# A fused trunk block: the output projection's rows split in place in a two-slot ring, the values of two head pairs copied together

## The chip, the cores and the metric

The kernel runs on one core of a Trainium2 chip. The metric is the device time of one execution in microseconds (us). Five engines work side by side, each through its own instructions in the order in which they stand in the program: TensorE (PE; its weight loads are listed apart as PEld), VectorE (DVE), ScalarE (ACT), GpSimd (POOL) and SyncE (SP), which in this kernel issues nearly all transfers. An instruction that waits holds up everything behind it on its engine.

## The reference

One layer over 1024 tokens of width 1024, all in float32. A normed input is projected, three mixers work on parts of the result, their outputs are joined and projected again, and a gated feed-forward part follows:

```python
h = rmsnorm(x, ln1[l]); z = h @ w_in[l]
y_pool, y_gla, y_fox = pool_mixer(...), gla_mixer(...), fox_mixer(...)
x = x + concat([y_pool, y_gla, y_fox]) @ w_o[l]
gate, up = split(rmsnorm(x, ln2[l]) @ w_gu[l])
x = x + (silu(gate) * up) @ w_down[l];  return rmsnorm(x, ln_f)
```

`fox_mixer` is a causal softmax attention with 8 heads of 64 columns. To each score a bias F_t - F_s is added, where F is a running sum of forget gates along the tokens; each head has its own row F.

## The kernel before

Every product keeps float32 accuracy with three matmuls: each operand is split into a high part (an ACT copy that rounds to fp32r) and a low part (a DVE or POOL subtraction, raw minus high), and high x high, high x low and low x high are summed in PSUM. So each block of weights costs a load, a copy and a subtraction before PE can use it.

The stages in order: norm and transposition of x (`hT`), the gated linear attention and the pooling (`Gla`, `pool_tile`), the attention (`fox_...`), the output projection in two halves (`pxa`, `pxb`, by `out_proj`), the feed-forward part (tiles `m`, L775), its down projection (tiles `d`, L1031), the last norm.

**The attention** works on four pairs of heads, p = 0 to 3. `fox_values(q)` (L518) projects the values for two pairs at once: 8 token blocks, `psv`, each 24 matmuls into a bank of the ring "gm", which has two banks, and then copies. `fox_qk(p)` projects queries and keys of one pair (`zq`, `zk`: 48 matmuls each in two banks "gm"). `fox_attend(p)` (L628) loads the bias row of each of the two heads, broadcast over 128 partitions (`fb`, L632), and then takes 8 items, a head `a` with two query blocks `m`: scores `s` on PE (three banks), bias and minimum by one DVE operation (L581), exponential on ACT (L585), scaling by POOL and DVE (L591, L593), transposition on PE (`pt`, L602), split on ACT and DVE (`pp`, L604 and L605), product with the values on PE (`o`, L616), sum of the two halves (L619, L622).

**The output projection's weights** are split early: `keep_wo(k)` (L280) loads 128 rows of `w_o` (512 KB), splits them and stores both parts to DRAM (`wod`); `fetch_wo` reads them back much later, for `out_proj`. In the Python text the eight calls stand between `fox_values(0)` and `fox_qk(0)`.

**Memory.** SBUF is cut into slots of 128 x 1024 floats. 33 of them go round as a queue: `G(name)` takes the slot that was freed longest ago, `free` puts slots back. The others form rings, from which `R(name, tag)` takes the next slot by turns: "p" 6, "pp" 3, "fb" 2, "wr" 2 (raw weights), "w" 4 (split weights). A tile that gets a slot waits until all users of the tile before it there are done. The ring "fb" holds the biases, and before the attention the norm's scratch and the rounded mixer outputs `mh`. `keep_wo` takes three tiles by `G` per call (raw, high, low), so that several calls can be under way at once.

**What sets the order.** The Python text gives the data flow and a priority. A scheduler of the tile framework lays all instructions out in advance, engine by engine, with its own estimate of durations; on the chip each engine then follows that fixed list. So a step can stand in the list far from its place in the text, and a change in one place moves others.

Of the kernel before, what the change touches and what calls it, by code (L numbers as in the profile page):

```python
# [10 lines left out]
F32R = mybir.dt.float32r  # L11
I8 = mybir.dt.int8
AF = mybir.ActivationFunctionType
ALU = mybir.AluOpType
# [4 lines left out]
P = 128  # L19
# [12 lines left out]
def tile_hybrid_block(ctx: ExitStack, tc, x, w_fv, w_gv, w_zt, w_o, w_gu, w_down, ln, w_pool, w_a3, chans, b_f, consts, out):  # L32
    nc = tc.nc
    ACT, DVE, POOL, PE, SP = nc.scalar, nc.vector, nc.gpsimd, nc.tensor, nc.sync
# [15 lines left out]
    def G(name, dtype=F32):  # L50
        i = idle.pop(0)
        t_ = big.tile([P, 1024], dtype, tag=f"g{i}", name=name)
        where[name] = i
        return t_

    def free(*names):
        for n in names:
            idle.append(where.pop(n))

    def R(name, dtype=F32, tag="p"):  # L60

        i = rings[tag].pop(0)
        rings[tag].append(i)
        return big.tile([P, 1024], dtype, tag=f"g{i}", name=name)
# [4 lines left out]
    def f(ap):  # L69
        return ap.bitcast(F32)  # L70
# [41 lines left out]
    def PS(tag, name):  # L112
        return pst.tile([P, 512], F32, tag=tag, name=name, bufs=BANKS[tag])
# [12 lines left out]
    def load_g(src, name, n=1024, eng=None, tag="wr"):  # L126
        if tag in rings:
            raw, own = R(f"{name}r", tag=tag), False
        else:
            raw, own = G(f"{name}r"), True  # L130
        r = split_w(src, raw, G(f"{name}h", F32R), G(f"{name}l", F32R), n, eng or DVE)
        if own:
            free(f"{name}r")
        return r
# [82 lines left out]
    for tb in range(NT):  # L217
# [4 lines left out]
        ps = PS("gm", f"psg{tb}")  # L222
# [45 lines left out]
    wod = dpool.tile([8, P, 2, D], F32, name="wod")  # L268
# [10 lines left out]

    def keep_wo(k):  # L280

        hi, lo = load_g(w_o[k * P:(k + 1) * P, :], f"wos{k}", tag="G")
        SP.dma_start(wod[k, :, 0], f(hi))
        SP.dma_start(wod[k, :, 1], f(lo))
        free(f"wos{k}h", f"wos{k}l")

    def fetch_wo(k):
        hl = G(f"wo{k}h", F32R), G(f"wo{k}l", F32R)
# [228 lines left out]

    def fox_values(q, smalls=((),) * NT):  # L518

        V = [[G(f"v{2 * q + j}_{i}", F32R).rearrange("p (t h s e) -> p t h s e", t=4, h=2, s=2) for i in range(2)] for j in range(2)]  # L520
        ws = [load_w(w_fv[:, q, i * 1024:(i + 1) * 1024], f"wfv{q}_{i}", eng=POOL) for i in range(2)]
        for tb in range(NT):
            ps = PS("gm", f"psv{q}_{tb}")
            woven(ps[:, 0:256], [(tok(hT, k, tb), tuple(w_[:, (k % 4) * 256:(k % 4) * 256 + 256] for w_ in ws[k // 4]))
                                 for k in range(NK)], smalls[tb])
            for j in range(2):
                v_ = V[j][tb // 4][:, tb % 4]
                pv = ps[:, 128 * j:128 * j + 128].rearrange("p (h e) -> p h e", h=2)
                ACT.activation(v_[:, :, 0], pv, AF.Copy)
                DVE.tensor_tensor(out=v_[:, :, 1], in0=pv, in1=f(v_[:, :, 0]), op=ALU.subtract)  # L530
        return V

    def fox_qk(p):
# [15 lines left out]

    def fox_item(p, a, m, ops, fb, V, Y):  # L550

        Q, K, KL = (t_[a] for t_ in ops)
        nm = f"{p}_{a}_{m}"
        rows = slice(64 * a, 64 * a + 64)
        Pb, Ws = [], []
        l, rl = S(f"l{nm}", 2), S(f"rl{nm}", 2)
        for i in range(2):
            qb = 2 * m + i
            W = P * (qb + 1)
            nh = 1 if W <= 512 else 2  # L560
            w = W // nh
            qs = slice(qb * P, (qb + 1) * P)
            mn = S(f"mn{nm}_{i}")
            if m >= 2:
                pb = R(f"pb{nm}_{i}")
            elif i == 0:
                pb2 = R(f"pb{nm}")
                pb = pb2[:, 0:512]
            else:
                pb = pb2[:, 512:1024]  # L570
            top = 3.0e38
            for h in range(nh):
                s = PS("s", f"s{nm}_{i}_{h}")
                ks = slice(h * w, (h + 1) * w)
                last = h == nh - 1
                PE.matmul(s[:, 0:w], Q[:, qs], K[:, ks], start=True, stop=False)  # L576
                PE.matmul(s[:, 0:w], Q[:, qs], KL[:, ks], start=False, stop=not last)  # L577
                if last:
                    PE.matmul(s[:, w - P:w], identr, maskr, start=False, stop=True)
                t_ = mn if last else S(f"mw{nm}_{i}")  # L580
                DVE.tensor_tensor_reduce(out=pb[:, ks], in0=s[:, 0:w], in1=fb[:, ks], scale=1.0, scalar=top,  # L581
                                         op0=ALU.add, op1=ALU.min, accum_out=t_)
                top = t_[:, 0:1]

            ACT.activation(pb[:, 0:W], pb[:, 0:W], AF.Exp, bias=mn[:, 0:1], scale=-1.0, accum_out=l[:, i:i + 1])  # L585
            Pb.append(pb)
            Ws.append(W)
        DVE.reciprocal(rl, l)  # L588
        for i, (pb, W) in enumerate(zip(Pb, Ws)):
            if i == 0:  # L590
                POOL.tensor_tensor(out=pb[:, 0:W], in0=pb[:, 0:W], in1=rl[:, 0:1].broadcast_to([P, W]), op=ALU.mult)  # L591
            else:
                DVE.tensor_scalar(out=pb[:, 0:W], in0=pb[:, 0:W], scalar1=rl[:, 1:2], scalar2=None, op0=ALU.mult)  # L593
        o = PS("o", f"o{nm}")
        for n in range(m + 1):
            pt = PS("pt", f"pt{nm}_{n}")
            pp = R(f"pp{nm}_{n}", F32R, tag="pp")
            cut = P if n == m else 0
            for b in range(2):
                for i in range(b if cut else 0, 2):  # L600
                    o0 = 256 * b + P * i - cut * b
                    PE.transpose(pt[:, o0:o0 + P], Pb[i][:, (2 * n + b) * P:(2 * n + b + 1) * P], ident)  # L602
            w = 512 - cut
            ACT.activation(pp[:, 0:w], pt[:, 0:w], AF.Copy)  # L604
            DVE.tensor_tensor(out=pp[:, 512:512 + w], in0=pt[:, 0:w], in1=f(pp[:, 0:w]), op=ALU.subtract)  # L605
            for b in range(2):
                kb = 2 * n + b
                o0 = cut * b
                v_ = V[p % 2][kb // 4][:, kb % 4, a]
                ph = pp[:, 256 * b:512 - o0] if b else pp[:, 0:256]  # L610
                pl = pp[:, 768:1024 - o0] if b else pp[:, 512:768]
                both = (o[:, o0:256], v_.rearrange("p s e -> p (s e)"), ph)
                high = (o[0:64, o0:256], v_[:, 0], pl)
                last = kb == 2 * m + 1
                for n_, args in enumerate((high, both) if last else (both, high)):
                    PE.matmul(*args, start=(kb == 0 and n_ == 0), stop=(last and n_ == 1))  # L616
        tmp = half(f"ot{nm}")
        ot, oy = tmp[0:64, 0:256], tmp[:, 256:512]
        ACT.activation(ot, o[64:128, 0:256], AF.Copy)  # L619
        if p < 3:  # L620
            oy = Y[:, m * 256:(m + 1) * 256]
        DVE.tensor_tensor(out=oy[rows], in0=o[0:64, 0:256], in1=ot, op=ALU.add)  # L622
        if p == 3:
            hi, lo = (last_mix[m // 2][rows, h, (m % 2) * 256:(m % 2 + 1) * 256] for h in range(2))
            ACT.activation(hi, oy[rows], AF.Copy)
            POOL.tensor_tensor(out=lo, in0=oy[rows], in1=f(hi), op=ALU.subtract)

    def fox_attend(p, ops, V, Y):  # L628
        fbs = []
# [4 lines left out]
        for a, m in ([(a, m) for a in range(2) for m in range(4)] if p < 3 else [(a, m) for m in (1, 0, 3, 2) for a in range(2)]):  # L634
            fox_item(p, a, m, ops, fbs[a], V, Y)

# [38 lines left out]
    V = fox_values(0, (B.within(1), o_[0][:1], o_[0][1:], o_[1][:1], o_[1][1:] + B.turned(0), B.turned(1), (), ()))  # L675
# [4 lines left out]
    for p in range(4):  # L680
        if p == 3:
            last_mix += [G(f"mix7_{g}", F32R).rearrange("p (h t) -> p h t", h=2) for g in range(2)]
        Y = G(f"y{p}") if p < 3 else None
        fox_attend(p, ops, V, Y)
        done = [f"{n}{p}_{a}" for n in ("q", "k", "kl") for a in range(2)] + [f"v{p}_{i}" for i in range(2)]
        if p == 1:
            V = fox_values(1)
            free(*[done.pop() for _ in range(2)])
        if p < 3:
            ops = fox_qk(p + 1)  # L690
        if p == 2:
            free(*names_T("hT"))
        if p < 3:
            free(*done)
            keep_mix(4 + p, Y)
            free(f"y{p}")
# [19 lines left out]
    raw = [[G(f"hr{q}_{kp}").rearrange("p (k t) -> p k t", k=2) for kp in range(2)] for q in range(4)]  # L716
# [407 lines left out]
```

## Time and profile before

| | |
|---|---|
| median of 3 runs | 1177.61 us (1175.17 to 1178.79) |
| the profiled execution | 1177.97 us |
| its span, first to last instruction | 1176.0 us |
| PE busy | 1136.7 us, 97% |
| DVE, ACT, POOL busy | 823.9, 537.0, 339.7 us |
| mean granted clock of PE | 0.992 |

The profile is one execution. A row of the timeline gives start, duration, engine, source line, operation and, in brackets, how long the engine sat idle before it and what ended the wait. A row of the table by windows gives a stretch of time and the busy time of each engine in it with its number of instructions, then the granted clock of PE, the share of the DMA engines that was busy, and GB/s. A DMA row gives the size and the median time from issue to landing.

### The profile page before, as it was taken

To read this page: it belongs to the slowest core of one execution; us is meant where nothing else is said; L and a number is where in the kernel's file an instruction comes from. 1 tells how busy PE (TensorE), PEld (TensorE's weight loads), DVE (VectorE), ACT (ScalarE), POOL (GpSimd) and SP (SyncE) were. 2 spreads that over 40 slices of the span, in tenths; PEclk is the share of its full clock that TensorE was granted. 3 is DMA by queue.
4 is the path that set the end of the run, shared out by engine and by line. 5 is a ranking of instruction groups with operands and counts; after the bars stand their busy time and mean duration, and the time that the engine had idled before them with its cause. 6 is when DMAs were issued, how large, how long until landed. Compare 5 with 4: busy or idle time off the path is not lost.

```text
span 1176.0 us, 15954 instructions
## 1 busy us (share of the span) xinstructions
PE 1136.7 (97%) x5928; PEld 959.4 (82%) x5928; DVE 823.9 (70%) x1365; ACT 537.0 (46%) x972; POOL 339.7 (29%) x260
## 2 busy tenths in 40 slices
PE   6999998999999999998999999999999999999996
PEld 6877878889978888886888888888888888888885
DVE  7596364287746866579997768777776684976686
ACT  6453344366654644456453434443343344334344
POOL 2131122443322313110202221022202271660693
PEclk9999999999999999999999999999999999999999
DMA  7111179311203734431333232332324688333233
GB/s 250 36 37 37 37 264 351 102 37 37 91 18 122 308 127 158 163 127 37 107 100 134 88 128 69 119 121 95 109 80 152 215 323 291 107 96 105 80 118 143
DMA packets 57692, 150.45 MB, mean 128 GB/s; under 512 B 5080, under 2 KB 5512, under 8 KB 57616
## 3 DMA queue, kind: packets, MB, share of 16 engines
q1 hardware_dynamic: 57184, 147.87, 36.8%
q0 software_dynamic: 432, 1.57, 0.4%
q8 instruction: 46, 0.75, 0.3%
q14 instruction: 30, 0.25, 0.1%
HBM read 105.09 MB, written 44.34 MB: 127 GB/s over the span
## 4 chain that ended last, share of the span: by engine, by line
PE 81%; DVE 7%; DMA 5%; POOL 3%; issue 2%; ACT 1%; SPq 0%; POOLq 0%; ACTq 0%; DVEq 0%
PE m L775 35%; PE d L1031 13%; PE pxa L144 4%; PE pxb L144 3%; PE o L616 3%; PE psv L152 2%; PE pt L602 2%; POOL rw L873 2%; PE s L576 1%; PE s L577 1%; PE zq3p L152 1%; PE psg L144 1%; PE zgk1p L152 1%; PE zgg0p L152 1%; PE zq2p L152 1%
## 5 line engine op out<-in xcount | busy, mean ns | idle before, releaser
L775 PE MATMUL m<-hA_0h,wr 128*128 128x512 f32 x616 | 214.2, 391 | 0.9 <-ACT hr L730 0.9
L775 PE MATMUL m<-hA_1h,wr 128*128 128x512 f32 x616 | 214.6, 389 | 0.0
L775 PEld LDWEIGHTS m<-hA_0h,wr 128*128 128x128 f32 x616 | 116.0, 188 | 25.3 <-ACT hr L730 1.4
L775 PEld LDWEIGHTS m<-hA_1h,wr 128*128 128x128 f32 x616 | 115.7, 188 | 23.9
L757 ACT ACTIVATE wr<-ws 128x512 fp32r<-128x512 f32 x110 | 69.2, 631 | 120.6 <-DVE ws L756 61.9
L775 PE MATMUL m<-hA_0l,wr 128*128 128x512 f32 x308 | 120.2, 390 | 0.7 <-DVE hA_0l L905 0.7
L1031 PE MATMUL d<-lw,ha 128*128 128x512 f32 x308 | 119.8, 389 | 0.0
L775 PE MATMUL m<-hA_1l,wr 128*128 128x512 f32 x308 | 119.8, 389 | 0.0
L1031 PE MATMUL d<-hw,ha 128*128 128x512 f32 x308 | 119.3, 389 | 0.0
L1031 PE MATMUL d<-hw,la 128*128 128x512 f32 x308 | 118.4, 389 | 0.0
L827 POOL TENSOR_TENSOR cg<-cu,cu 128x512 f32<-128x512 f32 x11 | 19.7, 1793 | 304.9 <-DVE cu L804 268.6
L758 DVE TENSOR_TENSOR wr<-ws,wr 128x512 fp32r<-128x512 f32 x110 | 75.6, 694 | 26.9 <-ACT wr L757 26.8
L881 DVE TENSOR_TENSOR la<-ra,ha 128x1024 fp32r<-128x1024 f32 (+1 forms) x42 | 57.5, 1375 | 30.1 <-ACT ha L880 22.4
L873 POOL TENSOR_TENSOR rw<-wd,wd 128x512 f32<-128x512 f32 x33 | 59.6, 1833 | 48.0 <-PE d L1031 47.9
L591 POOL TENSOR_TENSOR pb<-pb,rl 128x128 f32<-128x128 f32 (+3 forms) x32 | 39.3, 1232 | 115.2 <-DVE rl L588 105.1
L880 ACT ACTIVATE ha<-ra 128x1024 fp32r<-128x1024 f32 (+1 forms) x42 | 41.2, 987 | 65.6 <-DMA ra<-cd 60.6
L775 PEld LDWEIGHTS m<-hA_0l,wr 128*128 128x128 f32 x308 | 58.0, 188 | 13.2 <-DVE hA_0l L905 1.1
L585 ACT ACTIVATE pb<-pb,mn 128x128 f32<-128x128 f32 (+3 forms) x64 | 49.5, 774 | 41.1 <-DVE mn L581 39.8
L605 DVE TENSOR_TENSOR pp<-pt,pp 128x512 fp32r<-128x512 f32 (+1 forms) x80 | 50.1, 631 | 25.7 <-ACT pp L604 25.5
L775 PEld LDWEIGHTS m<-hA_1l,wr 128*128 128x128 f32 x308 | 57.8, 188 | 12.1
L1031 PEld LDWEIGHTS d<-hw,ha 128*128 128x128 f32 x308 | 57.8, 188 | 12.1
L1031 PEld LDWEIGHTS d<-hw,la 128*128 128x128 f32 x308 | 57.8, 188 | 12.1
(399 smaller groups left out, 2699.1 us busy)
## 6 DMA issues: line engine op xcount, KB each, us to landing
ra<-cd SPq DMA_DIRECT2D x35, 512.0 KB, 3.9
wu<-in_w_gu_dram SPq DMA_DIRECT2D x22, 512.0 KB, 4.8
wg<-in_w_gu_dram SPq DMA_DIRECT2D x22, 512.0 KB, 3.7
wd<-in_w_down_dram SPq DMA_DIRECT2D x22, 512.0 KB, 6.7
mix<-mixs SPq DMA_DIRECT2D x14, 512.0 KB, 6.1
cd<-cg SPq DMA_DIRECT2D x11, 512.0 KB, 6.4
cd<-cs SPq DMA_DIRECT2D x11, 512.0 KB, 3.4
cd<-cu SPq DMA_DIRECT2D x11, 512.0 KB, 3.4
```

The lines of the kernel that those rows point to most:

```text
L144: PE.matmul(ps, a, b, start=(n == 0), stop=(n == last))
L152: PE.matmul(ps, a, b, start=(i == 0 and n == 0), stop=(i == len(terms) - 1 and n == 2))
L585: ACT.activation(pb[:, 0:W], pb[:, 0:W], AF.Exp, bias=mn[:, 0:1], scale=-1.0, accum_out=l[:, i:i + 1])
L591: POOL.tensor_tensor(out=pb[:, 0:W], in0=pb[:, 0:W], in1=rl[:, 0:1].broadcast_to([P, W]), op=ALU.mult)
L605: DVE.tensor_tensor(out=pp[:, 512:512 + w], in0=pt[:, 0:w], in1=f(pp[:, 0:w]), op=ALU.subtract)
L757: ACT.activation(hi, src, AF.Copy)
L758: DVE.tensor_tensor(out=lo, in0=src, in1=f(hi), op=ALU.subtract)
L775: PE.matmul(ps, a, b, start=(n == 0), stop=(n == 11))
L873: POOL.tensor_tensor(out=raw_[:, j * 512:j * 512 + 512], in0=wd[h0, j0 + j][:, e0, :], in1=wd[h1, j0 + j][:, e1, :], op=op)
L880: ACT.activation(hi[:, sl], src, AF.Copy)
L881: DVE.tensor_tensor(out=lo[:, sl], in0=src, in1=f(hi[:, sl]), op=ALU.subtract)
L1031: PE.matmul(banks[t], a[:, o], b[:, ns], start=(j0 + j == 0 and m == 0), stop=(j0 + j == NF // 2 - 1 and m == 2))
```

## The change

Two edits. `keep_wo` takes its tiles from the ring "fb" of two slots in place of the queue of 33: raw always gets one slot and the high part the other, and the low part is written over raw. The calls stay where they are in the text. And `fox_values` lays the values of its two pairs side by side in four shared tiles, so that each token block is copied by one ACT and one DVE operation of 128 x 256 in place of two of 128 x 128 on each. The four tiles are freed after the second of the two pairs; before, each pair had two tiles of its own, freed with the pair.

```diff
     def keep_wo(k):
-        hi, lo = load_g(w_o[k * P:(k + 1) * P, :], f"wos{k}", tag="G")
+        raw, hi = R(f"wos{k}", tag="fb"), R(f"wosh{k}", F32R, tag="fb")
+        SP.dma_start(raw, w_o[k * P:(k + 1) * P, :])
+        ACT.activation(hi, raw, AF.Copy)
+        DVE.tensor_tensor(out=raw, in0=raw, in1=f(hi), op=ALU.subtract)
         SP.dma_start(wod[k, :, 0], f(hi))
-        SP.dma_start(wod[k, :, 1], f(lo))
-        free(f"wos{k}h", f"wos{k}l")
+        SP.dma_start(wod[k, :, 1], raw)
...
     def fox_values(q, smalls=((),) * NT):
-        V = [[G(f"v{2 * q + j}_{i}", F32R).rearrange("p (t h s e) -> p t h s e", t=4, h=2, s=2) for i in range(2)] for j in range(2)]
+        V = [G(f"v{q}_{i}", F32R).rearrange("p (t j h s e) -> p t j h s e", t=2, j=2, h=2, s=2) for i in range(4)]
...
-            for j in range(2):
-                v_ = V[j][tb // 4][:, tb % 4]
-                pv = ps[:, 128 * j:128 * j + 128].rearrange("p (h e) -> p h e", h=2)
-                ACT.activation(v_[:, :, 0], pv, AF.Copy)
-                DVE.tensor_tensor(out=v_[:, :, 1], in0=pv, in1=f(v_[:, :, 0]), op=ALU.subtract)
+            v_ = V[tb // 2][:, tb % 2]
+            pv = ps[:, 0:256].rearrange("p (j h e) -> p j h e", j=2, h=2)
+            ACT.activation(v_[:, :, :, 0], pv, AF.Copy)
+            DVE.tensor_tensor(out=v_[:, :, :, 1], in0=pv, in1=f(v_[:, :, :, 0]), op=ALU.subtract)
...
-                v_ = V[p % 2][kb // 4][:, kb % 4, a]
+                v_ = V[kb // 2][:, kb % 2, p % 2, a]
...
-        done = [f"{n}{p}_{a}" for n in ("q", "k", "kl") for a in range(2)] + [f"v{p}_{i}" for i in range(2)]
+        done = [f"{n}{p}_{a}" for n in ("q", "k", "kl") for a in range(2)] + [f"v{p // 2}_{i}" for i in range(4) if p % 2]
         if p == 1:
             V = fox_values(1)
-            free(*[done.pop() for _ in range(2)])
+            free(*[done.pop() for _ in range(4)])
```

The scheduler lays the program out anew. Lines from L283 on shift by up to three in the changed kernel (the bias load L632 is L633 there, the scores L576 are L577). Three places matter.

First, SP's queue before the first pair of heads. In the kernel before, the loads `wos` run several at a time, and the bias of pair 0's first head (the first `fb`) is loaded while the second part of the first block is still to be stored:

```order
L117 DMA zq0r<-in_w_zt_dram 128x1024
L117 DMA wos0r<-in_w_o_dram 128x1024
L275 DMA mixs<-mh_1405 128x1024
L276 DMA mixs<-pa_1106 128x1024
L283 DMA wod<-wos0h 128x1024
L632 DMA fb_0_2066<-Fd 128x1024
L284 DMA wod<-wos0l 128x1024
L117 DMA wos3r<-in_w_o_dram 128x1024
L117 DMA wos1r<-in_w_o_dram 128x1024
```

In the changed kernel, the same place, from the first block on (`wos` is raw and then the low part, `wosh` the high part; 1843 is block 0, 1850 block 1):

```order
L283 DMA wos_1843<-in_w_o_dram 128x1024
L117 DMA zk0r<-in_w_zt_dram 128x1024
L275 DMA mixs<-mh_1782 128x1024
L276 DMA mixs<-gy_1379 128x1024
L117 DMA zq1r<-in_w_zt_dram 128x1024
L286 DMA wod<-wosh_1844 128x1024
L287 DMA wod<-wos_1843 128x1024
L117 DMA zk1r<-in_w_zt_dram 128x1024
L283 DMA wos_1850<-in_w_o_dram 128x1024
L286 DMA wod<-wosh_1851 128x1024
L287 DMA wod<-wos_1850 128x1024
```

and at the end of the eight blocks (1885 is block 6, 1892 block 7):

```order
L117 DMA zk2r<-in_w_zt_dram 128x1024
L283 DMA wos_1885<-in_w_o_dram 128x1024
L286 DMA wod<-wosh_1886 128x1024
L287 DMA wod<-wos_1885 128x1024
L283 DMA wos_1892<-in_w_o_dram 128x1024
L286 DMA wod<-wosh_1893 128x1024
L287 DMA wod<-wos_1892 128x1024
L633 DMA fb_1_2044<-Fd 128x1024
L633 DMA fb_0_2042<-Fd 128x1024
```

The blocks now follow one another, and both biases of pair 0 come behind the last of them; the weights `zk1`, `wfv` of the second two pairs, `zq2` and `zk2` are loaded in between, ahead of the biases.

Second, PE where the first pair's scores begin to need a fourth bank. Before (names with numbers; `s0_0_1_1` is the fourth tile of scores), it stands inside the projection `zq1`:

```order
L152 MATMUL zq1p1_2579<-hT1_1_0_91,zq1h_2545 128x512
L152 MATMUL zq1p1_2579<-hT1_1_1_92,zq1h_2545 128x512
L576 MATMUL s0_0_1_1_0_2116<-k0_0_1925,q0_0_1923 128x512
L577 MATMUL s0_0_1_1_0_2116<-kl0_0_1927,q0_0_1923 128x512
L579 MATMUL s0_0_1_1_0_2116<-maskr_74,identr_73 128x128
L576 MATMUL s0_0_2_0_0_2156<-k0_0_1925,q0_0_1923 128x320
L577 MATMUL s0_0_2_0_0_2156<-kl0_0_1927,q0_0_1923 128x320
L152 MATMUL zq1p1_2579<-hT1_1_0_91,zq1l_2546 128x512
L152 MATMUL zq1p1_2579<-hT1_1_0_91,zq1h_2545 128x512
```

Now it stands behind the whole of `zq1` and `zk1` and behind two of the eight blocks of the second two pairs' values, `psv1_0` and `psv1_1`:

```order
L152 MATMUL psv1_1_3177<-wfv1_1l_3146,hT3_0_0_97 128x256
L152 MATMUL psv1_1_3177<-wfv1_1h_3145,hT3_0_1_98 128x256
L577 MATMUL s0_0_1_1_0_2092<-k0_0_1901,q0_0_1899 128x512
L578 MATMUL s0_0_1_1_0_2092<-kl0_0_1903,q0_0_1899 128x512
L580 MATMUL s0_0_1_1_0_2092<-maskr_74,identr_73 128x128
L577 MATMUL s0_0_2_0_0_2132<-k0_0_1901,q0_0_1899 128x320
L578 MATMUL s0_0_2_0_0_2132<-kl0_0_1903,q0_0_1899 128x320
L577 MATMUL s0_0_2_0_1_2137<-k0_0_1901,q0_0_1899 128x320
L578 MATMUL s0_0_2_0_1_2137<-kl0_0_1903,q0_0_1899 128x320
L580 MATMUL s0_0_2_0_1_2137<-maskr_74,identr_73 128x128
```

The projections that stood between the scores stand ahead of them now.

Third, ACT at the copies of those value blocks. Before, they stand in the second head's items, and each block takes two copies:

```order
L604 ACTIVATE pp0_0_3_1_2267<-pt0_0_3_1_2266 128x512
L585 ACTIVATE pb0_1_2_0_2389,l0_1_2_2386<-pb0_1_2_0_2389,mn0_1_2_0_2388 128x640
L529 ACTIVATE v2_0_3158<-psv1_0_3174 128x2x64
L585 ACTIVATE pb0_1_2_1_2402,l0_1_2_2386<-pb0_1_2_1_2402,mn0_1_2_1_2401 128x768
L529 ACTIVATE v3_0_3160<-psv1_0_3174 128x2x64
```

In the changed kernel they stand in the first head's:

```order
L605 ACTIVATE pp0_0_1_0_2103<-pt0_0_1_0_2102 128x512
L620 ACTIVATE ot0_0_0_2078<-o0_0_0_2066 64x256
L586 ACTIVATE pb0_0_3_0_2201,l0_0_3_2198<-pb0_0_3_0_2201,mn0_0_3_0_2200 128x896
L605 ACTIVATE pp0_0_1_1_2115<-pt0_0_1_1_2114 128x384
L530 ACTIVATE v1_0_3134<-psv1_0_3150 128x4x64
L530 ACTIVATE v1_0_3134<-psv1_1_3177 128x4x64
L605 ACTIVATE pp0_0_2_0_2161<-pt0_0_2_0_2160 128x512
```

The tile `v1_0` gets the slot of pair 0's keys `k0_0`, so its copies wait for that head's last scores, and until then both banks "gm" are taken and PE's list has no further projection.

## Prediction

> **What bounds the kernel now.** I read the page's first lines, then PE's idle time on the timeline, then the stretch from 150 to 355 us, where the change works.
>
> ```profile
> span 1176.0 us, 15954 instructions
> PE 1136.7 (97%) x5928; PEld 959.4 (82%) x5928; DVE 823.9 (70%) x1365; ACT 537.0 (46%) x972; POOL 339.7 (29%) x260
> ```
>
> PE is busy for all but 39 us, and nothing in the change alters its matmuls. So the change moves the time only by what it does to PE's gaps. The table by windows shows the stretch in three parts (us from:to, length, then busy time of PE, PEld, DVE, ACT, POOL, then PE's clock, DMA share, GB/s):
>
> ```profile
> 163.90:206.10 42.20, 36.33 (x316) 33.78 (x314) 21.94 (x45) 15.83 (x32) 8.99 (x4) 0.96 0.89 315
> 206.10:231.40 25.30, 25.26 (x115) 21.06 (x116) 5.54 (x9) 7.64 (x11) 9.87 (x9) 1.00 0.30 94
> 231.40:354.50 123.10, 119.81 (x802) 108.94 (x800) 86.40 (x217) 74.28 (x161) 43.98 (x39) 1.00 0.16 48
> ```
>
> In the first part the values of pairs 0 and 1 are projected and the eight `wos` blocks go through; PE idles 5.9 us and its clock is 0.96. In the second come `zq0` and `zk0`. In the third, the attention of pairs 0 and 1 runs interleaved with `zq1`, `zk1`, `psv1`, `zq2`, `zk2`, and PE idles 3.3 us in 123. DVE is at 70% there, so the interleaved projections hide what the attention's chains wait for.
>
> PE's gaps and ACT's on the timeline (start, duration, in brackets the idle time before it and what ended it):
>
> ```profile
> 176.25 0.35 PE L152 MATMUL psv<-wfv_0h,hT 128*128 128x256 f32 x1 [2.17 <-DVE v L530]
> 198.04 0.39 PE L152 MATMUL psv<-wfv_0h,hT 128*128 128x256 f32 x1 [1.56 <-DVE v L530]
> 206.14 0.70 PE L152 MATMUL zq0p<-hT,zq0h 128*128 128x512 f32 x2 [1.14 <-DVE v L530]
> 354.49 1.16 PE L152 MATMUL zq3p<-hT,zq3h 128*128 128x512 f32 x2 [2.55 <-DVE kl L545]
> 170.60 1.06 ACT L118 ACTIVATE wos3h<-wos3r 128x1024 fp32r<-128x1024 f32 x1 [5.91 <-DMA wos3r<-in_w_o_dram]
> 195.47 1.06 ACT L118 ACTIVATE wos7h<-wos7r 128x1024 fp32r<-128x1024 f32 x1 [2.86 <-DMA wos7r<-in_w_o_dram]
> ```
>
> The first two gaps are the blocks' doing: ACT stood in its list at a `wos` copy whose load had not landed, the copies of `psv` queued behind it, and PE had no bank.
>
> **The gain.** In the changed order no `wos` copy stands among the copies of `psv0`, so these two gaps go: 2.17 + 1.56 = 3.7 us. The first also cost clock:
>
> ```profile
> 170.00:180.00 10.00, 7.83 (x68) 7.58 (x67) 4.55 (x8) 3.00 (x6) 0.00 (x0) 0.85 0.76 204
> 350.00:360.00 10.00, 7.10 (x28) 5.43 (x26) 5.38 (x8) 3.30 (x6) 4.55 (x6) 0.83 0.26 105
> ```
>
> 0.85 over 10 us is 1.5 us of clock lost, and the first part's 0.96 over 42.2 us is 1.7; the same follows the gap of 2.55 us at 354. I take 1.7 us a time. The Trainium skill's page "TensorE: Matmul & The Clock Gate", in "What's actually happening", has the clock halved after at least one idle window of about 3.4 us; by that a gap of 2.17 us would cost no clock and the gain would be 3.7 us. The trace differs, so I keep 1.7. The gap of 1.14 us before `zq0` stays: its weights' slot is freed by the last values, in both orders. Gain: 3.7 + 1.7 = 5.4 us, so `zq0` runs from 206.14 - 5.4 = 200.7.
>
> **The joined copies.** 128 x 128 against the nearest rows of 128 x 256:
>
> ```profile
> L529 ACT ACTIVATE v<-psv x32: 255/272/278, 172.8 to 314.5; 128x128 fp32r<-128x128 f32 x32
> L451 ACT ACTIVATE on<-po x8: 375/384/387, 123.9 to 190.8; 128x256 f32<-128x256 f32 x8
> L530 DVE TENSOR_TENSOR v<-psv,v x32: 269/283/292, 175.2 to 315.2; 128x128 fp32r<-128x128 f32 x32
> L457 DVE TENSOR_TENSOR on<-po,gn_r x8: 411/418/424, 127.2 to 195.3; 128x256 f32<-128x256 f32 x8
> ```
>
> ACT does 16 x 0.384 in place of 32 x 0.272 us, 2.6 us less; DVE 16 x 0.418 in place of 32 x 0.283, 2.4 us less. Neither engine ends PE's waits here, except by the two gaps counted above, so I count 0; both ends of this lie between 0 and 2.6 us of gain.
>
> **The ring of two.** Raw and high part take both slots of "fb", so a block's load waits until the store of the block before has landed. Eight rounds of load, copy, subtraction and store stand in a row, and the biases of pair 0 behind them, because they use the same slots. Rows for a round:
>
> ```profile
> 195.47 1.07 ACT wos7h L118
> 196.56 1.23 DVE wos7l L119
> zk2r<-in_w_zt_dram SPq DMA_DIRECT2D x1, 512.0 KB, 3.6
> zq3r<-in_w_zt_dram SPq DMA_DIRECT2D x1, 512.0 KB, 3.4
> zk1r<-in_w_zt_dram SPq DMA_DIRECT2D x1, 512.0 KB, 5.4
> wod<-wos4h SPq DMA_DIRECT2D x1, 512.0 KB, 2.7
> wod<-wos3h SPq DMA_DIRECT2D x1, 512.0 KB, 3.3
> wod<-wos0l SPq DMA_DIRECT2D x1, 512.0 KB, 3.8
> fb<-Fd SPq DMA_DIRECT2D x2, 512.0 KB, 3.7
> 199.97 1.23 DVE L274 TENSOR_TENSOR gy<-gy,mh 128x1024 f32<-128x1024 f32 x1 [0.93 <-ACT mh L273]
> 204.44 1.06 ACT L118 ACTIVATE zk0h<-zk0r 128x1024 fp32r<-128x1024 f32 x1
> ```
>
> The subtraction in place takes as long as the other (L274's, with the same shape, 1.23 us), so 0 for that. I take the load at 3.6 us, since the DMA engines are at 0.16 to 0.30 in the second and third part and not at 0.89, copy and subtraction at 2.3, the store at 3.3, and 0.2 for the handovers: 9.4 us. Ends: 3.4 + 2.3 + 2.7 + 0.2 = 8.6 and 5.4 + 2.3 + 3.8 + 0.2 = 11.7. [...]
>
> When does it start? ACT's first `wos` copy now stands behind that of `zk0`, which ran at 204.44 to 205.50 before and so runs 199.0 to 200.1. Copy and subtraction end at 202.4, the store goes at 202.5, and seven more rounds put the last store at 202.5 + 7 x 9.4 = 268.3. Store and bias: 268.3 + 3.3 + 3.7 = 275.3. ACT's list adds some: the fifth to seventh copies stand between those of `zq1` and `zk1`, which wait for PE and for each other, some 2.5 us (estimate). So DVE can take the first scores at about 277.8, where before it did at:
>
> ```profile
> 231.38 0.29 DVE L581 CUSTOM_DVE_ANT_0 pb<-s,fb 128x128 f32<-128x128 f32 x1
> 206.14 10.71 PE zq0p L152 x46
> 216.85 10.88 PE zk0p L152 x48
> 228.14 2.96 PE zq1p L152 x13
> 198.04 6.03 PE psv L152 x48
> ```
>
> **What PE has until then.** The other four rows are of the chain of waits and give the length of a projection (13 matmuls of `zq1` were done before the first scores were taken). Ahead of the fourth bank of scores the changed list has `zq0`, `zk0`, `zq1`, `zk1`, two blocks `psv1` and some scores (1.2 us): 10.71 + 3 x 10.88 + 6.03 + 1.2 = 50.6 us, to 200.7 + 50.6 = 251.3. The `wos` copies in ACT's list hold up the copies of `zq1` and `zk1` (a copy waits for its load, which comes every 9.4 us, and PE wants a bank every half projection, 5.4), which I put at 3 us: 254. There PE stops: three score banks are full and DVE lacks the bias, both banks "gm" hold values that wait for the keys' slot. It waits until 277.8, that is 23.8 us.
>
> **The attention after that.** PE has left of the third part: 119.8 less `zq1` (35 of 48 matmuls, 8.0), `zk1` 10.9, `psv1` 6.0 and the scores done, 94 us. DVE has 86.4 less the copies of `zq1`, `zk1` and the rest, some 79. So PE bounds it still, but with less to interleave: the first head's first two items have no projection between them until `psv1_2`, and the last head's `pt` and `o` have none at the end, since `zk2` is through. I add 4 and 3 us for these (estimates from DVE's share of a head, some 70 of the 79 us over four heads, 17 to 18, against PE's (94 - 21.8 for `zq2` and `zk2` - 18 for six blocks) / 4 = 13.5) and 1.7 of clock after the long wait: 103 us, with 96 and 110 as ends. Pair 2 begins at 277.8 + 103 = 380.8, where before it began at 354.5 and then lost 1.7 of clock. The difference is 380.8 - 354.5 - 1.7 = 24.6 us. The rest of PE's, DVE's and SP's lists is nearly the same row by row, so I carry this to the end: 0 there.
>
> Counted by PE's gaps it is 23.8 + 3 + (103 - 94) - 5.4 - 3.3 - 1.7 = 25.4, which agrees. From the profiled execution's 1177.97 (2.0 more than its span, 0.4 more than the median): 1177.97 + 24.6 = 1202.6, so 1203 us.
>
> **The rivals.**
>
> *Faster (0.03).* The rounds end before PE runs dry, and only the gain remains: 1178.0 - 5.4 = 1172.6. It decides at 254 us: seven rounds would have to take (254 - 202.5 - 7) / 7 = 6.4 us each. Load, copy and subtraction alone are 3.4 + 2.3 = 5.7, so nothing speaks for it. No change (0.03), with rounds near 7 us, or with the scheduler's list filled in some way I do not see, has the same against it.
>
> *A shorter wait (0.14).* Quick rounds (8.6) put the first scores at 202.5 + 60.2 + 2.7 + 3.6 = 269, and the attention packs to 96 us: 365, that is +9: 1187 to 1194. For it: the DMA engines are nearly idle there, and PE can run without a gap beside a DVE that is as full as that:
>
> ```profile
> 250.00:260.00 10.00, 10.00 (x64) 8.90 (x64) 8.12 (x21) 7.12 (x17) 5.03 (x6) 1.00 0.18 54
> 260.00:270.00 10.00, 10.00 (x81) 9.81 (x80) 8.82 (x23) 7.83 (x17) 6.10 (x7) 1.00 0.17 54
> ```
> Against it: loads of `zq1` to `zk2` fall between the rounds.
>
> *A longer one (0.14).* Other loads in flight stretch the rounds: at 11.7 the first scores come at 202.5 + 81.9 + 3.8 + 5.4 = 294, +40 or more: 1215 to 1226. Or the clock drops time and again in an attention with gaps, at 1.7 us for each gap of over 2 us: five of them are +8.5, 1211. The Trainium skill's page "TensorE: Matmul & The Clock Gate", by the section named above, would have such drops only after gaps of about 3.4 us.
>
> *Not what it says (in the first).* The split is "one at a time", but not in its old place: it goes on beside four projections. Had the list kept the old place, PE would wait for all eight rounds before `zq0`; the list shows that it doesn't.
>
> **How the numbers follow.** The forecast (1194 to 1215) has 0.66, the two neighbours 0.14 each, the others 0.06. The range takes most of both neighbours: 1187 to 1224. A measurement can tell about 0.3% (3.5 us) from no change. Slower 0.94, same 0.03, faster 0.03.
>
> **What would show it.** In the changed profile: no gaps of PE on `v` between 164 and 200 and `zq0` some 5 us earlier; `wos` loads about 9.4 us apart from 206 on; one gap of PE of 15 to 30 us ahead of the first pair's scores, ended by DVE's L582 and behind it the `fb` load; the first L582 at 270 to 290; an attention of pairs 0 and 1 of some 100 us with DVE near 80%; equal lengths from pair 2 on. It is wrong if that gap is under 5 us, or if PE's gaps lie in the feed-forward part.

## The result, and the profile after

The changed kernel takes 1219.11 us (median of 4 runs, 1217.88 to 1219.55), the kernel before 1177.8 us on the same chip: a ratio of 1.0358, 95% interval 1.0342 to 1.0374. The profiled execution took 1218.81 us. The page of the changed kernel begins:

```profile
span 1217.0 us, 15904 instructions
PE 1144.9 (94%) x5928; PEld 964.9 (79%) x5928; DVE 826.7 (68%) x1349; ACT 534.8 (44%) x956; POOL 337.8 (28%) x260
```

The span is 41.0 us longer, PE's busy time 8.2 us: most of the loss is idle time of PE, the rest its clock. First starts from the trace show where the loss arises:

| first | before | after | gained or lost on the way there |
|---|---|---|---|
| `psv` on PE | 163.9 | 162.3 | -1.6 |
| `zq0` on PE | 204.3 | 195.5 | -7.2 |
| scores taken by DVE | 231.4 | 276.2 | +53.6 |
| `zq3` on PE (pair 2's attention begins) | 354.5 | 387.4 | -11.9 |
| `pxa` on PE | 398.1 | 431.1 | +0.1 |
| `pxb` on PE | 470.5 | 508.9 | +5.4 |
| the last `m` with `hA_0h` | 955.2 | 996.2 | +2.6 |

So 33 us are lost ahead of pair 2, and 8 more from the start of `pxa` on, in the output projection and at its end. The table by windows of the changed kernel, with the stretches that answer to those shown of before:

```profile
162.30:195.50 33.20, 33.20 (x315) 31.89 (x313) 11.80 (x23) 6.88 (x15) 5.72 (x4) 1.00 0.08 23
195.50:250.00 54.50, 47.68 (x216) 38.32 (x214) 19.84 (x22) 21.15 (x28) 23.00 (x20) 1.00 0.60 210
250.00:276.20 26.20, 6.98 (x35) 6.81 (x35) 3.39 (x4) 3.40 (x3) 1.89 (x3) 0.57 0.62 217
276.20:387.40 111.20, 100.42 (x667) 92.32 (x667) 83.04 (x202) 65.62 (x142) 31.81 (x25) 0.95 0.12 43
```

The values of the first two pairs are now projected without a gap and at full clock. Then PE works 47.7 of 54.5 us, and in the next 26.2 us only 7.0, while no other engine has much work (DVE 3.4 us). The main waits of PE on the timeline of the changed kernel:

```profile
197.89 0.50 PE L152 MATMUL zq0p<-hT,zq0l 128*128 128x512 f32 x1 [0.56 <-POOL zq0l L119]
239.39 0.70 PE L152 MATMUL zk1p<-hT,zk1h 128*128 128x512 f32 x2 [1.74 <-DVE q L541]
251.12 0.55 PE L152 MATMUL psv<-wfv_0h,hT 128*128 128x256 f32 x1 [4.47 <-DVE kl L546]
276.58 0.80 PE L577 MATMUL s<-k,q 128*128 128x512 f32 x1 [18.48 <-DVE mn L582]
286.55 0.63 PE L603 MATMUL pt<-ident,pb 128*128 128x128 f32 x4 [1.97 <-DVE pp L606]
372.37 1.39 PE L603 MATMUL pt<-ident,pb 128*128 128x128 f32 x8 [3.15 <-DVE pp L606]
384.47 0.67 PE L577 MATMUL s<-k,q 128*128 128x128 f32 x3 [1.81 <-POOL k L548]
387.38 1.22 PE L152 MATMUL zq3p<-hT,zq3h 128*128 128x512 f32 x2 [2.25 <-DVE kl L546]
513.26 0.71 PE L144 MATMUL pxb<-wo5h,mix 128*128 128x512 f32 x2 [1.87 <-DMA wo5h<-wod]
522.43 0.47 PE L144 MATMUL pxb<-wo6h,mix 128*128 128x512 f32 x1 [2.37 <-DMA mix<-mixs]
```

The long one ends when DVE has added the first bias. What DVE waits for is seen by going back along the timelines of SP, ACT and DVE (the second load `wos`, then the last round):

```profile
205.01 0.33 SPq L283 DMA_DIRECT2D wos<-in_w_o_dram  x1
...
262.97 0.33 SPq L283 DMA_DIRECT2D wos<-in_w_o_dram  x1
266.58 1.06 ACT L284 ACTIVATE wosh<-wos 128x1024 fp32r<-128x1024 f32 x1 [7.55 <-DMA wos<-in_w_o_dram]
...
268.92 0.32 SPq L287 DMA_DIRECT2D wod<-wos  x1
270.39 1.53 SPq L633 DMA_DIRECT2D fb<-Fd  x2
276.22 0.29 DVE L582 CUSTOM_DVE_ANT_0 pb<-s,fb 128x128 f32<-128x128 f32 x1 [7.34 <-DMA fb<-Fd]
```

The loads from the second to the eighth block are issued from 205.01 to 262.97, one every 58.0 / 6 = 9.66 us (8.7 to 11.8 us apart). The last store goes out at 268.9, the biases follow, DVE takes the first scores when they have landed. No step of this chain is long; they stand one behind another. The DMA table of the changed kernel gives one load and one store of a round:

```profile
wos<-in_w_o_dram SPq DMA_DIRECT2D x8, 512.0 KB, 3.6
wod<-wos SPq DMA_DIRECT2D x8, 512.0 KB, 2.7
```

The later 8 us are another matter: PE waits there for rows of `w_o` and mixed outputs that are fetched back (the last two rows of its waits above; with smaller waits for `mix` and `pp`, PE waits 6.6 us from `pxa` to the end of `pxb`, and 1.0 us before). The issue of the load `wo5h`, before and after:

```profile
L290 SPq DMA_DIRECT2D wo5h<-wod x1: 319/319/319, 435.8 to 435.8; - x1
```
```profile
L292 SPq DMA_DIRECT2D wo5h<-wod x1: 353/353/353, 505.6 to 505.6; - x1
```

Before, it was issued 35 us ahead of `pxb`; now 3 us ahead.

### The profile page after: what moved, and what is told of

The parts are those of the page before. It is cut to its first block, busy times and chain, and to the rows that moved or that the text cites. A ratio compares the mean times of both kernels' runs of the same rounds, so it can differ in the third digit from the quotient of the medians.

```text
span 1217.0 us, 15904 instructions
## 1 busy us (share of the span) xinstructions
PE 1144.9 (94%) x5928; PEld 964.9 (79%) x5928; DVE 826.7 (68%) x1349; ACT 534.8 (44%) x956; POOL 337.8 (28%) x260
## 4 chain that ended last, share of the span: by engine, by line
PE 61%; DMA 3%; DVE 2%; issue 1%; POOL 1%; ACT 0%; POOLq 0%; DVEq 0%; ACTq 0%
PE m L776 34%; PE d L1032 14%; PE pxb L144 3%; PE pxa L144 3%; DMA mix<-mixs 2%; PE zq3p L152 1%; PE pt L603 1%; PE o L617 1%; PE zk3p L152 1%; DMA wo5h<-wod 1%; PE n2pt L729 1%; PE s L578 0%; PE s L577 0%; DVE lw L882 0%; POOL f_r L107 0%
## 5 line engine op out<-in xcount | busy, mean ns | idle before, releaser
L1032 PEld LDWEIGHTS d<-lw,ha 128*128 128x128 f32 x308 | 57.8, 188 | 12.0
L1032 PEld LDWEIGHTS d<-hw,ha 128*128 128x128 f32 x308 | 57.8, 188 | 11.9
```

The lines of the kernel that those rows point to most:

```text
L1032: PE.matmul(banks[t], a[:, o], b[:, ns], start=(j0 + j == 0 and m == 0), stop=(j0 + j == NF // 2 - 1 and m == 2))
```

## The experiments

Theory A, from the prediction: pair 0's biases stand behind eight serial rounds in the two-slot ring, and that is the long wait. Rivals: B, the `wos` copies in ACT's and DVE's lists stop PE; C, the shared value tiles, held until the odd pair is done, make the wait. For the late loss there is theory D: the value tiles that are held longer keep slots from the rows of `w_o`, so these are fetched late. Ratios are against the kernel before on the same chip, with the 95% interval.

**1. The ring edit alone.** The kernel before with `keep_wo` as in the change and the values as before.

> Only the ring edit, the values copied pair by pair as before. Theory A (pair 0's biases stand behind eight rounds in a ring of two): the first L582 operation at 265 to 285 us, one gap of PE of 15 to 30 us ahead of it, PE's last waits before pxb as in the kernel before (about 2 us in all after 420), total 1208 to 1214 us, that is 5 to 10 under the changed kernel. Theory C (the value tiles that are held for two pairs make the gap): no gap over 5 us there, total 1172 to 1182.

1209.32 us, 1.0291 (1.0273 to 1.0310). The table of PE's waits has the long one nearly unchanged:

```profile
PE s L578 <- DVE mn L583: 19.9, 1, 19.9
```

The first scores come at 280.4, pair 2 begins at 389.0, and the output projection lasts as long as before (the matmuls of `pxb` with `wo4h` start from 504.3 to 564.7, 60.4 us; before, from 470.5 to 531.0). So the ring edit makes the early loss, and none of the late one.

**2. The joined values alone.** The kernel before with the second edit only.

> Only the joined values, the w_o rows split in slots of the big queue as before. Theory A: first scores taken at 228 to 233 us as before, no gap over 3 us there; the loads of wo4 and wo5 late, with 4 to 9 us of PE's waits and clock before the feed-forward part, total 1180 to 1188. Theory C: a gap of over 10 us ahead of or inside the attention, total over 1195.

1189.91 us, 1.0122 (1.0104 to 1.0140): a little over the range. There is no wait at the first scores (229.2, pair 2 at 354.3), which refutes C for the early loss; PE waits 1.9 us for `wo5h` and 2.9 us for `mix` in `pxb`, as in the changed kernel.

**3. Pair 0's biases outside the ring.** The changed kernel, with two slots of the big queue for these two tiles:

```diff
-            fb = R(f"fb{p}_{a}", tag="fb")
+            fb = G(f"fb{p}_{a}") if p == 0 else R(f"fb{p}_{a}", tag="fb")
...
+        if p == 0:
+            free("fb0_0", "fb0_1")
```

> The changed kernel, but the two biases of pair 0 lie in slots of the big queue, so they don't wait for the eight rounds; the rounds go on in the ring. Theory A: first scores at 222 to 235 us, no gap over 5 us ahead of them, total 1184 to 1195 (the late waits of the values stay). Theory B (what stops PE is the w_o copies standing in ACT's and DVE's lists, ahead of the copies that free banks): PE still loses 15 us or more between 220 and 300, now on copies of projections and of pt, total 1200 to 1215.

1185.02 us, 1.0087 (1.0069 to 1.0104). All eight rounds and their copies are still in the lists, yet DVE's first scores (the group of L582 that reads `fb`, first to last start) come 50 us earlier than in the changed kernel:

```profile
L582 DVE CUSTOM_DVE_ANT_0 pb<-s,fb x64: 270/552/692, 225.7 to 462.2; 128x384 f32<-128x384 f32 x16, 128x512 f32<-128x512 f32 x16, 128x128 f32<-128x128 f32 x8, 128x256 f32<-128x256 f32 x8
```

That is the test between A and B: the copies stayed, the wait went, and with it 2.7% of the time. A holds for the early loss.

**4. Half as many rounds.** The changed kernel, with blocks 4 to 7 split in two slots of the big queue each.

```diff
-        raw, hi = R(f"wos{k}", tag="fb"), R(f"wosh{k}", F32R, tag="fb")
+        if k < 4:
+            raw, hi = R(f"wos{k}", tag="fb"), R(f"wosh{k}", F32R, tag="fb")
+        else:
+            raw, hi = G(f"wos{k}"), G(f"wosh{k}", F32R)
```

> The changed kernel, but only blocks 0 to 3 go through the ring of two; blocks 4 to 7 take two slots each of the big queue (also split in place). Theory A: four rounds fewer, 4 x 9.5 = 38 us earlier: first scores at 236 to 246 us, gap under 8 us, total 1184 to 1196. Theory B: the four blocks outside come back among the copies of psv0 and cost 3 to 6 us there, and the gap stays over 10 us, total over 1200.

1191.16 us, 1.0138 (1.0118 to 1.0158). First scores at 241.7, 35 us earlier for four rounds fewer (four times 9.66 are 38.6), and pair 2 begins at 358.7. PE no longer waits long, since its other work lasts until then. The ring's length in rounds sets the time of the first scores.

**5. The hold alone.** The kernel before, values copied pair by pair; only their freeing is delayed to the end of the odd pair.

```diff
-        done = [f"{n}{p}_{a}" for n in ("q", "k", "kl") for a in range(2)] + [f"v{p}_{i}" for i in range(2)]
+        done = [f"{n}{p}_{a}" for n in ("q", "k", "kl") for a in range(2)] + [f"v{j}_{i}" for j in (p - 1, p) for i in range(2) if p % 2]
...
-            free(*[done.pop() for _ in range(2)])
+            free(*[done.pop() for _ in range(4)])
```

> The kernel before, values copied pair by pair as before; only the freeing of the value tiles is delayed, so that all four are held to the end of the odd pair. The joined copies alone came at 1.012 of before, and all of it was lost between the begin and the end of the second half of the output projection. Theory D (the loss is the hold: fewer slots are free while the rows wo4 to wo7 and the mixed outputs are to be fetched): 1183 to 1191 us against some 1175 before, the loads of wo4 to wo7 come late and together, pxb lasts 66 us in place of 60, pair 3's projection zq3 still begins at 354. Rival (the loss comes from the wider copy itself, another layout of the values or another list): 1173 to 1178, pxb 60 us. Prediction's step (neither costs anything): also 1173 to 1178.

1184.93 us, 1.0080 (1.0067 to 1.0094), with the same operations as before. The load `wo5h` is late as in the changed kernel, at the begin of `pxb` (475.1 here):

```profile
L290 SPq DMA_DIRECT2D wo5h<-wod x1: 354/354/354, 471.7 to 471.7; - x1
```

So value tiles that are freed one pair later cost 0.8% by themselves: D holds for this part. Expected were 66 us for `pxb`, from its first start to its last with `wo4h`; it took 61.6, and `pxb` began later (78.5 us behind `pxa`, against 72.4 before). Experiment 2 loses 0.4% more, some 5 us. The windows around `pxb` (476.00:553.00 of experiment 2, then 475.10:547.00 of this one) hold the same number of matmuls and differ by 5.1 us, of which 3.4 are idle time of PE and 1.7 busy time, at a granted clock of 0.96 and 0.98:

```profile
476.00:553.00 77.00, 67.67 (x331) 55.64 (x329) 46.80 (x64) 37.10 (x80) 10.35 (x19) 0.96 0.35 132
```
```profile
475.10:547.00 71.90, 65.92 (x331) 54.68 (x329) 47.20 (x65) 37.84 (x80) 11.31 (x19) 0.98 0.36 133
```

Experiment 3 copies its values as wide as experiment 2, and its like window, 476.90:548.90 with as many matmuls, is 72.0 us long. So the width does not make these 5 us; what does stays open.

**6. The values joined for pairs 0 and 1 alone.** Experiment 3, with the tiles of pairs 2 and 3 as before.

> The changed kernel with pair 0's biases outside the ring (that one came at 1.009 of before), and the values joined for pairs 0 and 1 alone; pairs 2 and 3 have their value tiles pair by pair as before. Theory D (the late loss is the hold of the second two pairs' value tiles through pair 3, ahead of the loads of wo4 to wo7): about the time of the ring edit with the biases outside, 1.000 to 1.003 of before, 1174 to 1179 us, with loads of wo4l and wo5h ahead of the last head and no wait of PE on wo5h. Rival (the wider copy itself or its layout costs): 1.006 to 1.010, 1182 to 1188.

1179.05 us, 1.0033 (1.0019 to 1.0046), against 1.0087 with all values joined. The load is early again:

```profile
L292 SPq DMA_DIRECT2D wo5h<-wod x1: 384/384/384, 432.6 to 432.6; - x1
```

The copies of pairs 0 and 1 are as wide as in the change, so a wide copy by itself does not make the late loss. This fits D, at the upper edge of its range (1.000 to 1.003). For pairs 2 and 3 this version leaves out both the wide copies and the hold; experiment 5 parts the two.

**7. The ring edit with the biases outside it**, values as before.

> The ring edit alone, with pair 0's two biases in slots of the big queue and the values as before. Theory A (the ring costs only by the biases behind it): the gain of 5.4 us shows that the prediction counted for the gaps at psv0, less what two more big slots taken cost: 1168 to 1176 us. Rival (the rounds cost something beside that, by copies that wait in ACT's list for their loads among the copies of zq1 and zk1): 1178 to 1190. First scores taken by DVE at 225 to 235 in both.

1177.87 us, 1.0017 (1.0001 to 1.0033), between the two ranges: the gain is missing. `zq0` begins at 197.4 with `psv` at 164.1, 33.3 us against 40.4, so 7.1 us are gained up to there, but pair 2 begins at 355.2, no earlier. In the attention (windows of this kernel) PE idles 8.3 us where it idled 3.3 before, and two rows of its timeline show one case:

```profile
164.10:197.40 33.30, 33.30 (x314) 31.83 (x312) 12.61 (x30) 7.94 (x22) 5.84 (x4) 1.00 0.17 58
226.90:355.20 128.30, 119.97 (x793) 107.78 (x791) 92.46 (x223) 77.98 (x166) 44.64 (x39) 1.00 0.32 107
```
```profile
251.27 1.06 ACT L284 ACTIVATE wosh<-wos 128x1024 fp32r<-128x1024 f32 x1 [1.72 <-DMA wos<-in_w_o_dram]
257.06 1.31 PE L618 MATMUL o<-pp,v 128*128 128x256 f32 x9 [1.80 <-DVE y L624]
```

ACT stands at a copy whose load has not landed, now among the attention's steps. Its exponentials come behind that copy, DVE's reciprocal waits for them (until 254.37), and PE waits for the `y` that follows. DVE's busy time in this stretch rose from 86.4 to 92.5 us. What was gained at `psv0` is lost again by the end of the attention.

**8. The splits moved, three big slots each as before.** Two places: four blocks behind each of the attentions of pairs 0 and 1; and all eight behind the first queries and keys.

```diff
-    for k in range(8):
-        keep_wo(k)
...
+        if p < 2:
+            for k in range(4 * p, 4 * p + 4):
+                keep_wo(k)
```

> The kernel before; only the place of the eight splits in the text is moved, four behind pair 0's attention and four behind pair 1's, with three big slots a block as before. If the two gaps at psv0 are worth what the prediction counted (3.7 us idle and 1.7 us of clock) and the splits find cover later: 1169 to 1173 us. If the slots they take later delay weights of pairs 2 and 3 or of the output projection: 1176 to 1190, with the waits of PE on loads of weights between 290 and 530.

> The kernel before; only the eight calls are moved behind the projection of pair 0's queries and keys, with three big slots a block as before. Gaps at psv0 gone: 1170 to 1174 us. If the copies then stop PE among zq1 and zk1 instead: 1175 to 1180, with gaps of PE on copies of z between 200 and 260.

The first: 1176.00 us, 1.0003 (0.9994 to 1.0012); the second: 1178.64 us, 1.0022 (1.0013 to 1.0031). In both PE reaches `zq0` after 33.4 and 34.0 us of `psv` in place of 40.4, and in both the attention from the first scores to `zq3` takes longer, 131.9 and 131.4 us against 123.1. So both came in the ranges of no gain, but the waits named with these, on loads of weights and on copies of projections, are not there: PE's longest is 2.9 us on `y` in the first, and in the second 2.5 us on the last copy ahead of `zq3`, as before, and 1.9 us on `pp`. In the first, DVE's subtraction of a block stands ahead of `y`:

```profile
222.40:354.30 131.90, 124.39 (x801) 111.76 (x800) 97.97 (x224) 79.81 (x167) 40.55 (x37) 0.97 0.43 149
```
```profile
269.60 2.00 DVE L593 TENSOR_SCALAR pb<-pb,rl 128x1024 f32<-128x1024 f32 x1
271.52 1.21 DVE L119 TENSOR_TENSOR wos0l<-wos0r,wos0h 128x1024 fp32r<-128x1024 f32 x1
272.84 0.42 DVE L622 TENSOR_TENSOR y<-o,ot 64x256 f32<-64x256 f32 x1
273.31 1.50 PE L616 MATMUL o<-pp,v 128*128 128x256 f32 x8 [2.92 <-DVE y L622]
```

**9. The same with POOL for the subtraction** (`eng=POOL` in `keep_wo`), to test theory E, that DVE's time in the attention takes the gain back.

> The kernel before with the eight splits moved behind the attentions of pairs 0 and 1 and their subtraction given to POOL. With DVE the gain of 7 us before zq0 was given back in the attention, in stretches in which DVE was 90% and more busy and ended PE's waits. Theory E (DVE's time in the attention is what took the gain back): DVE is spared some 8 x 1.23 = 9.8 us there and about half the gain stays: 1169 to 1173 us, 0.994 to 0.998 of before. Rival (ACT's copies or the loads' place in the queues took it back): 1175 to 1178, as with DVE.

> The kernel before with the eight calls behind the projection of pair 0's queries and keys, and their subtraction given to POOL. Theory E: 1170 to 1175 us, 0.995 to 0.999 of before, DVE under 90% between 240 and 300 us. Rival (ACT's copies took the gain back, or POOL's longer subtraction delays the keys' casts on POOL): 1177 to 1181, with gaps of PE on POOL's k or on pp by ACT.

1179.50 us, 1.0038 (1.0023 to 1.0052), and 1190.01 us, 1.0124 (1.0103 to 1.0145). Both lie above both of their ranges. Theory E in this form falls: both are slower than with DVE. At the same wait as above, in the first of the two kernels:

```profile
270.75 2.79 POOL L119 TENSOR_TENSOR wos0l<-wos0r,wos0h 128x1024 fp32r<-128x1024 f32 x1
271.45 2.25 DVE L593 TENSOR_SCALAR pb<-pb,rl 128x256 f32<-128x256 f32 x1
273.72 0.42 DVE L622 TENSOR_TENSOR y<-o,ot 64x256 f32<-64x256 f32 x1
274.20 1.48 PE L616 MATMUL o<-pp,v 128*128 128x256 f32 x8 [4.07 <-DVE y L622]
```

DVE is rid of 1.21 us and loses 1.9: the scaling of 128 x 256 (L593) takes 2.25 us beside POOL's subtraction, and ends 0.2 us after it. In the second kernel the largest stall ahead of pair 2 is one of 5.0 us, in which DVE's `y` waited until the store of a `wos` tile had landed:

```profile
261.86 0.42 DVE L622 TENSOR_TENSOR y<-o,ot 64x256 f32<-64x256 f32 x1 [3.51 <-DMA wod<-wos7h]
262.33 1.97 PE L616 MATMUL o<-pp,v 128*128 128x256 f32 x8 [4.99 <-DVE y L622]
```

**10. The splits beside `zq2` and `zk2`**, where DVE and the DMA engines had time: the eight calls stand behind `fox_values(1)`, with the kernel's own three slots each.

> The kernel before with all eight splits moved behind the values of pairs 2 and 3, with three big slots a block and DVE's subtraction as before, so that they run beside the projections zq2 and zk2 (310 to 354 us in the kernel before), where DVE was 33 to 65% busy and the DMA engines under 10%. Theory F (the 7 us gained before zq0 are given back only where the splits' ACT and DVE work stands among the attention's): beside the projections they cost nothing, so that the gain less a clock gate of 1.7 us stays: 1167 to 1172 us, 0.994 to 0.998 of before, with zq3 some 5 us earlier. Rival (PE has no work left to be pulled forward, so that a wait comes elsewhere, on wo0 or mix ahead of pxa or on the splits' slots ahead of zq3): 1174 to 1182, pxa no earlier than 398.

1204.19 us, 1.0235 (1.0221 to 1.0249): theory F falls, and by more than its rival allowed. Four blocks came one after another at the end, each load behind the store of the one before, and the copies of pair 2's keys behind them in DVE's list:

```profile
362.67 0.41 SPq L117 DMA_DIRECT2D wos5r<-in_w_o_dram  x1
369.73 1.06 ACT L118 ACTIVATE wos5h<-wos5r 128x1024 fp32r<-128x1024 f32 x1 [8.93 <-DMA wos5r<-in_w_o_dram]
...
372.07 0.32 SPq L284 DMA_DIRECT2D wod<-wos5l  x1
372.44 0.45 SPq L117 DMA_DIRECT2D wos7r<-in_w_o_dram  x1
...
380.57 2.70 DVE L545 TENSOR_TENSOR kl<-zk2p,k 64x512 fp32r<-64x512 f32 x4 [1.46 <-DMA wod<-wos7h]
382.81 1.19 PE L152 MATMUL zq3p<-hT,zq3h 128*128 128x512 f32 x2 [32.78 <-DVE kl L545]
```

It is a wait like the changed kernel's, in a queue of 33 slots: loads that each follow their predecessor's store, and something that PE needs behind the last. But here the load of `wos7` goes out 0.4 us after the store was issued, and the stores of that block took 2.6 us to land; so it waited for its turn in SP's list and not for the slot of the store before it. No version was faster than the kernel before.

## Why the prediction was right, and where it was not

The forecast was 1203 us for a profiled execution that took 1218.81. The sign, the cause and the place of the early loss were right; the sum is 16 us short. The time lies within the whole range (1187 to 1224), but above the 1194 to 1215 that had the main chance, among the times of the rival "a longer one". That rival's first condition, rounds stretched to 11.7 us, did not come about; its second, a clock that drops time and again, did in part.

**The gain** (5.4 us) was there: `psv` to `zq0` takes 33.2 us in place of 40.4, so 7.2. Of the stretch before,

```profile
163.90:204.30 40.40, 35.63 (x315) 33.52 (x313) 21.36 (x43) 14.53 (x30) 7.19 (x4) 0.96 0.88 311
```

4.8 us of idle time went, where the two largest gaps (3.7) were counted, and 2.4 us of busy time, where 1.7 of clock were counted. (The row at 206.14, from which the prediction starts `zq0`, is its third matmul; the first two ran from 204.3.) But the rival "faster" (1172.6) rested on this gain being kept, and experiments 7 and 8 show that it is not: with no bias in the way, all 7 us are lost again by pair 2.

**The ring of two**: a round was put at 9.4 us and took 9.66; the last store at 268.3 came at 268.9; the first scores at 277.8 came at 276.2. The path is shown by experiments 1, 3 and 4. That the size of a round fits so well is partly luck: the store was put at 3.3 us and took 2.7, and waits in the queues made up for it.

**What PE has until then**: it ran dry at 276.58 - 18.48 = 258.1, not at 254. It began earlier than forecast (the matmul that the prediction starts from at 196.6, not 200.7), but the stalls took 7.5 us (0.6, 0.7, 1.7 and 4.5) in place of 3, and the work 54.0 us in place of 50.6; 2.9 of these 3.4 us are the half clock from 250.1 to 256.9 (the rows of the last section). Stalls and the wait are 26.0 us together, where 26.8 were forecast. That these agree is luck: the earlier begin made up for the longer work.

**The attention after that** (103 us, up to 110) took 111.2. PE idles 10.8 us in it, where the prediction's terms for idle time were 4 + 3 = 7: about 2 us came at the first items, and 8 at the end of the last head. The prediction let the 3.3 us of idle time of before go, but 2.55 of these are the wait ahead of `zq3`, and that wait is still there (2.25). And the clock: 0.95 over 111.2 us is 5.6 us, where 1.7 were allowed for. Busy time without that loss is 94.9 us, as forecast (94). So this step was mis-sized, by 3.8 us of idle time and 3.9 of clock.

**"Rest 0" and "joined copies 0"** is the step that failed. The copies cost as forecast (medians of 0.384 us on ACT and 0.423 on DVE), but the edit also moves the freeing of pair 2's tiles behind pair 3. The description of the change names that, and the prediction gave it no price; in the changed kernel 8.0 us are lost from `pxa` on, and the hold by itself costs 0.8% (experiment 5).

From these: pair 2 began 6.6 us later than forecast (387.4 against 380.8), the 1.7 us of clock credited there did not come (the clock drops around the start of `zq3` in the changed kernel too), and the tail adds 8.0: 16.3, the whole difference.

The ratios of the two halves (1.0291 and 1.0122) multiply to 1.0417, over the 1.0358 of the change. On top of the ring edit the joined values cost less than alone: 1.0358 / 1.0291 = 1.0065, and with the biases outside (experiments 3 and 7) 1.0087 / 1.0017 = 1.0070. That is near the 1.0080 of the hold. What experiment 2 loses beyond the hold is not lost there; why was not tried.

## What to carry to other kernels

When tiles move into a small ring, look for who else draws on that ring behind them: here two 4-us loads of biases waited for eight rounds of 9.7 us. When tiles of different lifetimes are joined, price the hold: count the slots at the next stage that fetches ahead, even if the joined operations are cheaper. And a stall taken from one stage is a gain only if the work that went with it fits elsewhere; look at that stage's waits before counting it.

## What was not expected of the hardware

**PE's clock** fell to half around short waits, in stretches of 3.4, 6.8 and 20.5 us, whole multiples of about 3.4. Windows of the changed kernel: at the wait of 4.47 us, at the long wait, behind the waits of 1.97 and 3.15 us, and at the waits of 1.81 and 2.25 us ahead of `zq3`; then one of before, behind the 2.17 us in `psv0`:

```profile
250.10:256.90 6.80, 5.78 (x27) 5.81 (x28) 0.84 (x2) 0.00 (x0) 1.79 (x3) 0.50 0.89 289
260.30:280.80 20.50, 4.22 (x15) 4.03 (x16) 5.35 (x17) 5.66 (x12) 1.29 (x2) 0.50 0.47 170
287.60:291.00 3.40, 3.40 (x20) 3.40 (x18) 3.40 (x12) 1.91 (x4) 0.00 (x0) 0.51 0.23 88
373.00:376.40 3.40, 3.30 (x17) 2.93 (x16) 1.92 (x4) 1.92 (x4) 0.00 (x0) 0.50 0.02 5
386.70:393.50 6.80, 6.12 (x15) 4.85 (x16) 1.24 (x2) 0.00 (x0) 2.67 (x5) 0.50 0.52 186
```
```profile
177.10:180.50 3.40, 3.40 (x18) 3.40 (x18) 0.00 (x0) 0.00 (x0) 0.00 (x0) 0.50 1.05 259
```

PE was busy for 6.1 us of the stretch around `zq3`, at half the clock: some 3 us lost beside the waits. Other waits of this size, of 1.74 us ahead of `zk1` and of 1.87 us in `pxb`, were not followed by a drop; what decides it, no run here tells. The Trainium skill's page "TensorE: Matmul & The Clock Gate", in "What's actually happening", has a free-running window of about 3.4 us, with which these lengths agree; the one idle window of about 3.4 us that it asks for is more than the 2.17 and 1.97 us of idle time here.

**DVE beside POOL**: L593 on 128 x 256 took 2.25 us beside POOL's subtraction (experiment 9) and 0.33 us at its fastest in the same kernel. The Trainium skill's page "SBUF — State Buffer", in "Who interferes with whom", says that the two engines share a port pair, that a `tensor_scalar` of DVE, as this one is, can take it, and that whoever issues first then has it for the whole instruction while the other is blocked. The rows agree: POOL began first, and DVE's operation ends 0.2 us behind POOL's. So POOL was no free engine in the attention.
